# One stage of a decoder trunk: late half projections in other turns, fixed places and other queues for attention's operands, one more turn behind the head norm

## The chip, the cores and the metric

The kernel runs on one core of one Trainium2 chip, as one launch. The metric is the device time of that launch in microseconds (us). The engines are named as in the profile: PE (TensorE, matrix products), PEld (its weight loads), DVE (VectorE), ACT (ScalarE), POOL (GpSimd) and SP (SyncE, which only issues DMAs). Each engine works off its own list of instructions in order; an instruction whose operand isn't ready holds up all that stand behind it on that engine. DMAs are issued from the lists of SP, ACT and POOL, and run beside the engines.

## The reference: what is computed

One layer of a trunk, sequence 1024, width 1024. The part that matters here is the mixing: one input projection of the normed input, split into three groups of heads that are computed apart and projected back together.

```python
z = rmsnorm(h, norm_mix_g[l]) @ w_in[l]
a_q, a_f, a_i, a_g, b_q, b_k, b_v, c_in = jnp.split(z, splits, axis=-1)
o_a = hgrn2_mix(a_q, a_f, a_i, a_g, lbs[l], hgrn_gnorm_g[l])      # 4 heads of 128
o_b = dilated_window_mix(b_q, b_k, b_v)                           # 4 heads of 64, three windows
o_c, v_first = rwkv7_mix(c_in, ...)                               # 4 heads of 64
h = h + jnp.concatenate([o_a, o_b, o_c], axis=-1) @ w_out[l]
h = h + conv_glu_ffn(rmsnorm(h, norm_ffn_g[l]), ...)
h = h + sigmoid(rmsnorm(h, norm_ple_g[l]) @ ple_gate[l]) * (p[l] @ ple_proj[l])
return rmsnorm(h, final_norm_g)
```

HGRN2 is a gated linear recurrence; each head's output is normed by itself (root mean square over its 128 columns), then multiplied by a gate. The attention adds three dilated causal windows under one softmax.

## The kernel before, in words

All activations lie transposed, 128 channels by 1024 positions. A product in full precision is made as three products of rounded parts (`mm3`, L125 to L134): high part by high, low by high, high by low. A weight block arrives as `wraw`, ACT copies its high part (`whi`, L106), DVE or POOL subtracts to get the low part (`wlo`, L108).

**Stages.** `phase_mix` (L308) first does the norm, then RWKV together with most blocks of the input projection, then the stage with which this case deals (L314 to L328), and after it `phase_out`, the output projection (its products are named `dp`), and the gated MLP. In the stage four streams run interleaved: A is the HGRN heads 0 and 2, one after the other, B the heads 1 and 3, C the attention of the two pairs of heads (`swa`), F the three blocks of the input projection that were left over (`project_late`): block 29, which is attention's v for pair 1, block 19, the gate of head 2, and block 23, the gate of head 3.

**Turns.** Each stream is a generator. `interleave` (L68) goes through a string of letters, and each letter lets its stream go on to its next `yield`. The string has rounds: in round r comes C if r is in `TURNS` (0, 1, 3, 4, 6, 7 and so on), then A, then B from round 6 on, then F in the odd rounds below 14 (L326, L327). This gives the order in which the program is written down; a scheduler of the framework then lists it per engine by when it takes operands to be ready, and may move instructions past one another.

**An HGRN head** (`hgrn_head`, L971) has these turns: load of the gate f and of q (`zl<-z`, from SP); first factors; scores of level 0 (`hsc`, L1002); seven levels, each four products of 128 by 128 (`hsc`, L1023), a predicated copy (`hS`, L1025), products with the running gate (`qt` L1028, `hk` L1026) and a copy for the next level (`ks` on ACT, L1013); transposes of v and of the keys (`vt`, L1046 and L1052); states (`hkv` L1067, chained on DVE as `hst`); output (`hpo`, L1086 and L1088); the head norm: square on ACT, sum on DVE, power on POOL (`hrs`, L1098), product on DVE (`ho`, L1100). The last turn transposes the normed output on PE (`vt<-cst,ho`, L1106), multiplies with the gate and splits it into the operand of the output projection.

**Attention** (`swa`, L1113) handles a pair of heads in 10 turns: scores of a query block qb (`swq`, L1167), mask and minimum on DVE (`lg`, L1174), exponential on ACT (L1176), a turn later the transposes of the weights (`swt`, L1190), and after another one the products with v (`swo`, L1203). Its operands q, k, v come back from memory by three DMAs on POOL's list (`swa_load`); v is transposed into `sV` (L1150) before the first scores. The places for q, k, v and `sV` are four buffers under one tag, taken in turn by whichever tile comes next when one is free.

**Late projections.** One turn of F is a half of a block: 24 products of 128 by 512 into one small accumulator `zp`, scaled on DVE, stored by a DMA on SP's list. They need nothing of the other streams. After the sixth half the stream makes the operand tiles of the output projection, which take the places of the input projection's operands X, and splits what is done by then (`o_split`, `xh` on ACT and `xl` on DVE or POOL, L155 and L157).

All small accumulators of the stage (`zp`, `hsc`, `vt`, `hkv`, `hpo`, `swt`, `swo`, `swd`) share four buffers; `swq` and `dp` share two larger ones. The HGRN tiles share 11 buffers.

In the profile, the products in 32 bits (all but those with `whi` and `wlo`) leave two records each, so a row "x8" in the trace is four instructions.

Of the kernel before, what the change touches and what calls it, by code (L numbers as in the profile page):

```python
# [10 lines left out]
F32 = mybir.dt.float32  # L11
# [7 lines left out]
P = 128  # L19
T = 1024  # L20
# [47 lines left out]
def interleave(order, streams):  # L68

    live = dict(streams)  # L70
    while live:
        for s in order:
            if s in live and next(live[s], STOP) is STOP:
                del live[s]
# [5 lines left out]
class Trunk:  # L80
# [227 lines left out]
    def phase_mix(self):  # L308
        nc, tc = self.nc, self.tc
        self.mix_norm()  # L310
        with tc.tile_pool(name="slots", bufs=1) as slots:
            self.slots, self.NSLOT = slots, 8
            self.rwkv()
        self.O, self.done = None, []  # L314
        for p in (0, 1):
            self.o_split(6 + p)
        with tc.tile_pool(name="hg", bufs=1) as slots, tc.tile_pool(name="sw", bufs=1) as sp:
            self.slots, self.NSLOT = slots, 11
            self.hgrn_setup()
            self.sp = sp  # L320
            self.swmask = sp.tile([P, T], F32, name="swmask")
            nc.scalar.dma_start(self.swmask, self.a["swm"])
            A = chain(self.hgrn_head(0), self.hgrn_head(2))
            B = chain(self.hgrn_head(1), self.hgrn_head(3))
            order = []
            for r in range(36):  # L326
                order += "C" * (r in self.TURNS) + "A" + "B" * (r > 5) + "F" * (r % 2 and r < 14)  # L327
            interleave(order, {"A": A, "B": B, "C": self.swa(sp), "F": self.project_late(self.rest)})  # L328

    TURNS = [i * 33 // 22 for i in range(23)]  # L330

    def mix_norm(self):

# [637 lines left out]
    def hgrn_head(self, h):  # L971
        nc, mxp, par, spool = self.nc, self.mxp, self.par, self.spool
# [6 lines left out]
        q = self.zload(j0 + 1, self.slot)  # L979
        yield  # L980
        nc.vector.tensor_scalar(f, f, self.olb[:, h:h + 1], self.lb[:, h:h + 1], ALU.mult, ALU.add)
        k = self.slot("hk")
# [16 lines left out]
        for i in (0, 1):  # L999
            sc = mxp.tile([P, 4, P], F32, tag="mx", name=self.nm("hsc"))  # L1000
# [5 lines left out]
        def blocks(l):  # L1006
            n = 1 << (l - 1)
            return n, HT // n, ([HT + n, 2], [2 * n, 256 // n], [1, n])
# [9 lines left out]
        for l in range(1, 8):  # L1018
            n, nb, half = blocks(l)
            qq = view(qt, 0, *half)  # L1020
            sc = mxp.tile([P, 4, P], F32, tag="mx", name=self.nm("hsc"))
# [19 lines left out]

        V = self.slot("hV")
        for hf in (0, 1):
            pt = mxp.tile([P, HT], F32, tag="mx", name=self.nm("vt"))
            for c in range(4):
                nc.tensor.transpose(pt[:, c * P:(c + 1) * P], vc[:, hf * HT + c * P:hf * HT + (c + 1) * P], self.ident)  # L1046
            nc.scalar.copy(V[:, hf * HT:(hf + 1) * HT], pt)
        kt = self.slot("hkt")
# [8 lines left out]
        def at(cc, swap=False):  # L1057
            c = (4 + cc if cc < 4 else 7 - cc) ^ (4 if swap else 0)
            return slice(c * P, (c + 1) * P)

        for hf in (0, 1):
            pk = mxp.tile([P, 4, P], F32, tag="mx", name=self.nm("hkv"))
            for c in range(4):
                cc = hf * 4 + c
                if cc == 7:
                    break
                nc.tensor.matmul(pk[:, c, :], kt[:, at(cc, True)], V[:, at(cc)], start=True, stop=True)  # L1067
            for c in range(4):
# [12 lines left out]
        for hf in (0, 1):  # L1081
            po = mxp.tile([P, 4, P], F32, tag="mx", name=self.nm("hpo"))
            for c in range(4):
                cc = 7 - c if hf == 0 else c
                s = at(cc)
                nc.tensor.matmul(po[:, c, :], S[:, s], V[:, s], start=True, stop=cc == 0)  # L1086
                if cc:
# [11 lines left out]
        o3 = o.rearrange("p (c v) -> p c v", v=P)  # L1099
        nc.vector.tensor_tensor(o3, o3, rs.unsqueeze(2).broadcast_to([P, 8, P]), ALU.mult)  # L1100
        yield
        for hf in (0, 1):
            sl = slice((1 - hf) * HT, (2 - hf) * HT)
            pt = mxp.tile([P, HT], F32, tag="mx", name=self.nm("vt"))
            for c in range(4):
                nc.tensor.transpose(pt[:, c * P:(c + 1) * P], o3[:, hf * 4 + c, :], self.ident)  # L1106
            nc.vector.scalar_tensor_tensor(oa[:, sl], pt if hf else pt[:, ::-1], par[:, PC_GN + h:PC_GN + h + 1], oa[:, sl], ALU.mult, ALU.mult)
# [4 lines left out]

    def swa(self, sp):  # L1113

        pend, fin, load = [], None, self.swa_load(sp, 0)
        yield
        for p in (0, 1):
            d = load
            self.swa_values_in(d)
            for qb in range(10):  # L1120
                if fin:
                    self.swa_out(*fin)
                    fin = None
                if qb < 8:
                    cur = self.swa_scores(sp, d, qb)
                if qb > 1:
                    fin = self.swa_values(sp, d, *pend.pop(0))
                if 0 < qb < 9:
                    pend[-1:] = [self.swa_turn(sp, *pend[-1])]
                if qb < 8:  # L1130
                    pend.append((qb, *cur))
                if qb == 7 and p == 0:
                    load = self.swa_load(sp, 1)
                yield
        self.swa_out(*fin)

    def swa_load(self, sp, p):
        d = {"p": p}
        for i, n in enumerate("qkv"):
            d[n] = self.zload(24 + 3 * p + i, lambda n: sp.tile([P, T], F32, tag="sslot", name=self.nm(n), bufs=4),  # L1140
                              self.nc.gpsimd)
        return d

    def swa_values_in(self, d):
        nc, vc = self.nc, d["v"]
        V = self.sp.tile([P, T], F32, tag="sslot", name=self.nm("sV"), bufs=4)
        for hf in (0, 1):
            pt = self.mxp.tile([P, HT], F32, tag="mx", name=self.nm("vt"))
            for c in range(4):
                nc.tensor.transpose(pt[:, c * P:(c + 1) * P], vc[:, hf * HT + c * P:hf * HT + (c + 1) * P], self.ident)  # L1150
            nc.scalar.copy(V[:, hf * HT:(hf + 1) * HT], pt)
        d["V"] = V.rearrange("p (b c) -> p b c", c=P)

# [699 lines left out]
```

## Time and profile before

| | us |
|---|---|
| median of 3 runs (1495.39 to 1498.95) | 1496.69 |
| the profiled execution, its own time | 1496.24 |
| its span from first to last instruction | 1494.5 |
| PE busy | 1445.1 (97%) |
| DVE busy | 1097.8 (73%) |
| ACT busy | 634.5 (42%) |
| POOL busy | 446.6 (30%) |
| the 16 DMA engines moved | 167.83 MB, 112 GB/s on the mean |

The stage starts at about 433.7 us of the span, and the operands of the output projection are all there at about 649 us. How to read a row of the timeline: start, length, engine, line, operation, output<-inputs, shape, number of instructions merged, and in brackets how long the engine was idle before it and what ended that. "PEclk" is the clock that PE was granted, as a share of the full one.

### The profile page before, as it was taken

The page shows a single profiled execution, that of the slowest core. Times are in us where ns is not written, and L with a number is a line of the kernel's source. Part 1 is how long each engine was busy: PE and PEld are TensorE (multiplying, and loading weights), DVE is VectorE, ACT ScalarE, POOL GpSimd, SP SyncE. Part 2 cuts the span into 40 slices and gives each one's busy share as a digit, 9 for nine tenths or more (in the row PEclk, how much of TensorE's full clock was granted, in tenths as well). Part 3 has the DMA queues.
Part 4 walks back from the last instruction along what each step waited for, and adds up shares of the span by engine and source line. Part 5 has one row for each costly group of instructions (what it writes and reads, how often), then busy time and mean ns, then how long its engine had stood idle before and what let it go on. Part 6 is the DMA issues. An engine that isn't in the chain of part 4 may idle for free.

```text
span 1494.5 us, 20176 instructions
## 1 busy us (share of the span) xinstructions
PE 1445.1 (97%) x7416; PEld 1199.0 (80%) x7416; DVE 1097.8 (73%) x1650; ACT 634.5 (42%) x1121; POOL 446.6 (30%) x362
## 2 busy tenths in 40 slices
PE   8999999999989889999999999999999999999996
PEld 7888997888977677778878888888888888888775
DVE  7666455585648668736788888888888799777684
ACT  6531343213425635425454444444444444455542
POOL 3232432313412122112144554444554000002343
PEclk9999999999999989999999999999999999999998
DMA  6123112232152111165333333333332883351443
GB/s 219 58 92 99 43 56 72 72 99 63 43 179 74 42 73 57 43 229 194 127 110 98 103 106 106 106 106 106 106 106 81 313 298 97 105 164 42 139 157 106
DMA packets 79874, 167.83 MB, mean 112 GB/s; under 512 B 20064, under 2 KB 22240, under 8 KB 79776
## 3 DMA queue, kind: packets, MB, share of 16 engines
q1 hardware_dynamic: 65424, 145.44, 29.8%
q10 hardware_dynamic: 13264, 17.04, 3.4%
q0 software_dynamic: 1088, 4.06, 0.8%
q8 instruction: 58, 0.95, 0.3%
q14 instruction: 40, 0.33, 0.1%
HBM read 120.12 MB, written 46.40 MB: 111 GB/s over the span
## 4 chain that ended last, share of the span: by engine, by line
PE 84%; DVE 6%; issue 4%; POOL 2%; DMA 2%; ACT 1%; DVEq 0%; POOLq 0%; ACTq 0%; SPq 0%
PE bg L1325 16%; PE bv L1325 12%; PE dp L130 8%; PE dp L134 8%; PE dp L132 8%; PE bg L1626 7%; PE bv L1626 7%; PE hsc L1023 2%; DMA zl<-z 1%; PE swq L1167 1%; PE swo L1203 1%; POOL wlo L108 1%; PE bv L130 1%; PE bv L132 1%; PE swt L1190 1%
## 5 line engine op out<-in xcount | busy, mean ns | idle before, releaser
L130 PE MATMUL dp<-xh,whi 128*128 128x512 f32 x560 | 202.7, 406 | 1.1 <-ACT xh L374 1.1
L134 PE MATMUL dp<-xh,wlo 128*128 128x512 f32 x560 | 194.4, 391 | 2.0 <-POOL wlo L108 1.1
L132 PE MATMUL dp<-xl,whi 128*128 128x512 f32 x560 | 194.5, 391 | 0.4 <-DVE xl L375 0.3
L108 POOL TENSOR_TENSOR wlo<-raw,whi 128x512 fp32r<-128x512 f32 x84 | 138.0, 1662 | 77.8 <-ACT whi L106 77.8
L108 POOL TENSOR_TENSOR wlo<-wraw,whi 128x512 fp32r<-128x512 f32 x64 | 88.0, 1379 | 233.2 <-ACT whi L106 203.9
L1325 PE MATMUL bg<-t,whi 128*128 128x512 f32 x352 | 132.7, 389 | 0.0
L106 ACT CAST whi<-wraw 128x512 fp32r<-128x512 f32 x120 | 72.1, 617 | 132.7 <-PE dp L132 94.4
L134 PEld LDWEIGHTS dp<-xh,wlo 128*128 128x128 f32 x560 | 105.0, 188 | 25.0 <-POOL wlo L108 1.5
L130 PEld LDWEIGHTS dp<-xh,whi 128*128 128x128 f32 x560 | 104.5, 188 | 23.6 <-issue 3.8
L132 PEld LDWEIGHTS dp<-xl,whi 128*128 128x128 f32 x560 | 105.2, 188 | 21.8 <-DVE xl L375 1.4
L108 POOL TENSOR_TENSOR wlo<-s,whi 128x512 fp32r<-128x512 f32 x44 | 65.9, 1498 | 159.5 <-ACT whi L106 147.3
L1626 PE MATMUL bg<-t,whi 128*128 128x512 f32 x308 | 95.0, 389 | 0.0
L1626 PE MATMUL bv<-t,whi 128*128 128x512 f32 x308 | 94.8, 389 | 0.0
L106 ACT CAST whi<-raw 128x512 fp32r<-128x512 f32 x88 | 52.6, 619 | 97.4 <-PE bv L1325 49.0
L106 ACT CAST whi<-s 128x512 fp32r<-128x512 f32 x66 | 38.9, 620 | 120.7 <-PE bg L1325 113.3
L1325 PEld LDWEIGHTS bg<-t,whi 128*128 128x128 f32 x352 | 66.0, 188 | 13.6
L175 POOL TENSOR_TENSOR rst<-rst,mhalf 128x4 f32<-128x4 f32 (+1 forms) x9 | 9.8, 1088 | 223.4 <-DVE rst L173 223.4
L108 DVE TENSOR_TENSOR wlo<-wraw,whi 128x512 fp32r<-128x512 f32 x56 | 48.2, 863 | 34.8 <-ACT whi L106 32.4
L1622 ACT CAST t<-t 128x512 fp32r<-128x512 f32 x77 | 47.8, 622 | 47.8 <-PE bv L1626 34.8
L1626 PEld LDWEIGHTS bv<-t,whi 128*128 128x128 f32 x308 | 57.8, 188 | 12.1
L1626 PEld LDWEIGHTS bg<-t,whi 128*128 128x128 f32 x308 | 57.7, 188 | 12.0
L1325 PE MATMUL bg<-t,wlo 128*128 128x512 f32 x176 | 67.2, 389 | 0.0
(429 smaller groups left out, 3660.9 us busy)
## 6 DMA issues: line engine op xcount, KB each, us to landing
raw<-in_ffn_up_dram SPq DMA_DIRECT2D x44, 512.0 KB, 3.7
wraw<-in_w_in_dram SPq DMA_DIRECT2D x29, 512.0 KB, 3.6
z<-zst SPq DMA_DIRECT2D x19, 512.0 KB, 2.9
gb<-ct SPq DMA_DIRECT2D x33, 256.0 KB, 2.0
t<-gb SPq DMA_DIRECT2D x33, 256.0 KB, 2.8
t<-gt SPq DMA_DIRECT2D x33, 256.0 KB, 2.7
zl<-z SPq DMA_DIRECT2D x16, 512.0 KB, 3.5
wraw<-in_ple_gate_dram SPq DMA_DIRECT2D x16, 512.0 KB, 3.6
```

The source lines that it names most:

```text
L106: nc.scalar.copy(hi, src)
L108: eng.tensor_tensor(lo, src, hi.bitcast(F32), ALU.subtract)
L130: nc.tensor.matmul(ps[hf], wh, xh[hf], start=first, stop=False)
L132: nc.tensor.matmul(ps[hf], wh, xl[hf], start=False, stop=False)
L134: nc.tensor.matmul(ps[hf], wl, xh[hf], start=False, stop=last)
L1023: nc.tensor.matmul(sc[:, c, :], ks[:, c * P:(c + 1) * P], view(qt, c * P, [2 * n, 64 // n], [HT + n, 2], [1, n]), start=True, stop=True)
L1167: nc.tensor.matmul(pq[h][:, b:b + w], d["q"][hs, qb * P:nk], d["k"][hs, b:b + w], start=True, stop=True)
L1190: nc.tensor.transpose(pt[:, kb * P:(kb + 1) * P], lg[:, b + kb * P:b + (kb + 1) * P], self.ident)
L1203: nc.tensor.matmul(po[hs, :], d["V"][:, kb, hs], pT[h][:, kb * P:(kb + 1) * P], start=kb == 0, stop=kb == qb)
L1325: nc.tensor.matmul(ps, w[part == 2][:, s], X[k][part == 1], start=start and k == part == 0, stop=k == 3 and part == 2, skip_group_check=no ...
L1622: nc.scalar.copy(xh, x)
L1626: nc.tensor.matmul(ps[m], wt[part == 2][:, m * P:(m + 1) * P], (xh, xl)[part == 1], start=k == part == 0, stop=k == NK - 1 and part == 2)
```

## The change

The reads of the four streams stay what they were; their places in the order, the places of attention's operands and the queues of its loads are others:

- The F turns stand in rounds 0, 1, 5, 9, 13, 16 and 17 (`LATE`) in place of 1, 3, 5, 7, 9, 11 and 13.
- The head norm's last turn comes one `yield` later, so that a head takes one round more, and the string has 38 rounds.
- Attention's q, k, v and `sV` have a buffer of their own each (`sa`, `sb`, `sc`, `sd`; the second pair's k goes to `sc`, its q to `sa`, its v to `sb`). The second pair's k is loaded from POOL's list after query block 5 of the first pair, q from ACT's list and v from POOL's list after block 7. `sV` is made after the scores of the first query block for pair 0, and after those of the second for pair 1.
- The pools `hg` and `sw` are opened so that each of their tiles waits for the earlier users of its own bytes only.

```diff
-        with tc.tile_pool(name="hg", bufs=1) as slots, tc.tile_pool(name="sw", bufs=1) as sp:
+        with self.pool("hg") as slots, self.pool("sw") as sp:
...
-            for r in range(36):
-                order += "C" * (r in self.TURNS) + "A" + "B" * (r > 5) + "F" * (r % 2 and r < 14)
+            for r in range(38):
+                order += "C" * (r in self.TURNS) + "A" + "B" * (r > 5) + "F" * (r in self.LATE)
...
+    LATE = 0, 1, 5, 9, 13, 16, 17
...
         nc.vector.tensor_tensor(o3, o3, rs.unsqueeze(2).broadcast_to([P, 8, P]), ALU.mult)
         yield
+        yield
...
-        pend, fin, load = [], None, self.swa_load(sp, 0)
+        nc, pend, fin = self.nc, [], None
+        ds = {0: {"p": 0}, 1: {"p": 1}}
+        for n, tag in zip("qkv", ("sa", "sb", "sc")):
+            self.swa_load(ds[0], n, tag, nc.gpsimd)
         yield
         for p in (0, 1):
-            d = load
-            self.swa_values_in(d)
+            d = ds[p]
...
                     cur = self.swa_scores(sp, d, qb)
+                if qb == p:
+                    self.swa_values_in(d)
...
-                if qb == 7 and p == 0:
-                    load = self.swa_load(sp, 1)
+                if p == 0 and qb == 5:
+                    self.swa_load(ds[1], "k", "sc", nc.gpsimd)
+                if p == 0 and qb == 7:
+                    self.swa_load(ds[1], "q", "sa", nc.scalar)
+                    self.swa_load(ds[1], "v", "sb", nc.gpsimd)
...
-    def swa_load(self, sp, p):
-        d = {"p": p}
-        for i, n in enumerate("qkv"):
-            d[n] = self.zload(24 + 3 * p + i, lambda n: sp.tile([P, T], F32, tag="sslot", name=self.nm(n), bufs=4),
-                              self.nc.gpsimd)
-        return d
+    def swa_load(self, d, n, tag, eng):
+        d[n] = self.zload(24 + 3 * d["p"] + "qkv".index(n),
+                          lambda nm: self.sp.tile([P, T], F32, tag=tag, name=self.nm(nm), bufs=1), eng)
...
-        V = self.sp.tile([P, T], F32, tag="sslot", name=self.nm("sV"), bufs=4)
+        V = self.sp.tile([P, T], F32, tag="sd", name=self.nm("sV"), bufs=1)
```

On PE the two lists differ only between row 1606 and row 2180 of 5267, which is this stage; in front of and behind it they are word for word the same. The lines of the changed kernel are numbered higher by 1 up to L1100, and by up to 6 behind it. Three places show what moved.

The first is PE's list at the start of the stage: `yt` and `pg` are the last products of RWKV, `vt` with `sV`'s operand `zl_3698` the transposes of v for pair 0, `zp` the half projection. Before:

```order
L751 MATMUL yt_3665<-cst,sc_2353 128x128 x4
L755 MATMUL pg_3672<-sg_474,par 128x512
L1150 MATMUL vt_3705<-cst,zl_3698 128x128 x4
L1150 MATMUL vt_3711<-cst,zl_3698 128x128 x4
L1167 MATMUL swq_3718<-zl_3696,zl_3694 128x128
L1167 MATMUL swq_3719<-zl_3696,zl_3694 128x128
L130 MATMUL zp_3746<-xh_105,whi_3736 128x512
```

In the changed kernel, the same place:

```order
L752 MATMUL yt_3665<-cst,sc_2353 128x128 x4
L756 MATMUL pg_3672<-sg_474,par 128x512
L130 MATMUL zp_3716<-xh_105,whi_3706 128x512
L132 MATMUL zp_3716<-xl_106,whi_3706 128x512
L134 MATMUL zp_3716<-xh_105,wlo_3708 128x512
```

The first half projection (24 products) now stands right behind RWKV; behind it come the two scores and the transposes of v, then the second half projection, and only then the scores of head 0's level 0, ahead of which one half projection stood before.

The second place is PE's list where the first pair of attention ends and head 0's output begins: `swt` are transposes of the weights of query block 6, `swq` the first scores of pair 1, with k and q in its inputs (`zl_4396`, `zl_4394` before, `zl_4100`, `zl_4326` now). Before:

```order
L1190 MATMUL swt_4383<-cst,lg_4211 128x128 x4
L1190 MATMUL swt_4389<-cst,lg_4211 128x128 x3
L1167 MATMUL swq_4629<-zl_4396,zl_4394 128x128
L1167 MATMUL swq_4630<-zl_4396,zl_4394 128x128
L1167 MATMUL swq_4712<-zl_4396,zl_4394 128x256
L1167 MATMUL swq_4713<-zl_4396,zl_4394 128x256
L1086 MATMUL hpo_4401<-hV_4250,hS_3773 128x128
```

Now:

```order
L1196 MATMUL swt_4315<-cst,lg_4172 128x128 x4
L1173 MATMUL swq_4533<-zl_4100,zl_4326 128x128
L1196 MATMUL swt_4321<-cst,lg_4172 128x128 x3
L1087 MATMUL hpo_4331<-hV_4211,hS_3800 128x128
L1089 MATMUL hpo_4331<-hst_4248,qt_3771 128x128
```

One score product of pair 1 is left ahead of head 0's output; the other three come 80 rows and more behind it. Ahead of these pieces stood, before, the sixth half projection, the last two scores of pair 0 and 12 `swo`; now the two scores and 12 `swo` alone.

The load of that q is the third place. Before, k and v of pair 1 stood on POOL's list behind three pieces that split operands (`zl_800` is k, `zl_801` is v; q, `zl_799`, had gone far earlier):

```order
L157 TENSOR_TENSOR xl_833_4507<-oc_286_1640,xh_832_4506 128x512
L108 TENSOR_TENSOR wlo_1071_5630<-wraw_1065_5622,whi_1070_5628 128x512
L157 TENSOR_TENSOR xl_835_4509<-oc_567_3267,xh_834_4508 128x512
L502 DMA zl_800_4396<-z28_3663 128x1024
L502 DMA zl_801_4398<-z29_3745 128x1024
L1098 TENSOR_TENSOR hrs_817_4480<-hss_816_4477,mhalf_83 128x8
```

Now k takes the early place on POOL's list, and q stands on ACT's list, between copies for head 1's levels and the exponential of query block 7:

```order
L1014 COPY ks_778_4273<-hk_728_4024 128x2x32x8
L1014 COPY ks_796_4358<-hk_728_4024 128x2x16x16
L503 DMA zl_790_4326<-z27_3620 128x1024
L1182 ACTIVATE lg_781_4282,sden_716_3977<-lg_781_4282,sden_716_3977 128x1024
```

The load of q waits for the last scores of pair 0, whose buffer it takes, and ACT waits with it. The transposes of head 0's normed output (`vt<-cst,ho`), too, have moved on PE's list: before, they came after 14 `swo`, 16 `swt` and one level; now a half projection, another level and 16 `swo` more stand between head 0's output and them. Of the other two half projections the fourth stands between levels of head 1 as one did before, and the last behind head 1's transposes.

## The prediction

> **What bounds the kernel now.** I read the page first, then the busy time of each engine by windows in the stage that the change rewrites, then what PE waits for there, and last the single rows. The page:
>
> ```profile
> span 1494.5 us, 20176 instructions
> ...
> PE 1445.1 (97%) x7416; PEld 1199.0 (80%) x7416; DVE 1097.8 (73%) x1650; ACT 634.5 (42%) x1121; POOL 446.6 (30%) x362
> ```
>
> PE is busy for 97% of the span, and the change leaves its instructions as they are. What can be won is PE's idle time and the time in which it runs at a lowered clock. The windows of the stage (start:end, length, then each engine's busy time with its count, the granted clock, the DMA share, GB/s) show where these lie:
>
> ```profile
> 433.70:462.84 29.14, 23.52 (x123) 18.45 (x122) 20.09 (x43) 10.74 (x27) 6.23 (x7) 0.94 0.49 163
> 462.84:514.50 51.66, 51.54 (x338) 40.47 (x337) 35.19 (x70) 31.94 (x57) 7.47 (x6) 1.00 0.11 37
> 514.50:550.06 35.56, 24.81 (x199) 21.59 (x199) 18.75 (x32) 15.51 (x29) 9.71 (x9) 0.81 0.33 111
> 550.06:634.40 84.34, 78.03 (x634) 62.81 (x633) 69.60 (x134) 44.22 (x92) 18.52 (x15) 0.98 0.13 45
> ...
> 433.70:650.00 216.30, 191.66 (x1363) 154.59 (x1362) 150.81 (x289) 105.88 (x207) 46.07 (x39) 0.95 0.21 71
> ```
>
> The first and the third stretch hold the holes: 5.6 and 10.8 us idle of 24.6 in all. In the second PE never waits. The clock fell to half in four places:
>
> ```profile
> 445.60:449.00 3.40, 3.40 (x18) 3.40 (x18) 1.95 (x5) 0.40 (x2) 0.21 (x1) 0.50 0.99 314
> 524.10:530.90 6.80, 5.54 (x24) 4.63 (x25) 1.05 (x6) 0.88 (x4) 0.00 (x0) 0.50 0.25 103
> 541.20:548.00 6.80, 5.49 (x34) 5.29 (x36) 5.68 (x8) 1.24 (x2) 1.82 (x3) 0.50 0.01 2
> 575.30:578.70 3.40, 3.37 (x18) 2.74 (x19) 3.30 (x6) 0.27 (x1) 0.00 (x0) 0.50 0.08 14
> ```
>
> At half rate half of PE's busy time is lost: (3.40 + 5.54 + 5.49 + 3.37) / 2 = 8.9 us. Without any hole the stage would be 24.6 + 8.9 = 33.5 us shorter; no change of order can give more. PE's waits in the stage (us in total, times, longest):
>
> ```profile
> PE vt L1106 <- DVE ho L1100: 8.0, 3, 4.4
> PE swq L1167 <- DMA zl<-z: 5.3, 1, 5.3
> PE hsc L1002 <- DVE hk L984: 3.7, 1, 3.7
> PE hsc L1023 <- DVE qt L1028: 3.4, 4, 1.6
> ```
>
> **The change, part by part.** All sums are made against the profiled execution's own 1496.24 us; the median is 0.45 higher, and about 0.2% (3.0 us) is the least that a measurement tells from no change.
>
> *a. The start, up to the third half projection.* The same work stands ahead of it as before, but the second half comes ahead of level 0's scores and covers their wait.
>
> ```profile
> 435.14 0.50 PE L130 MATMUL zp<-xh,whi 128*128 128x512 f32 x1
> ...
> 440.48 0.39 PE L134 MATMUL zp<-xh,wlo 128*128 128x512 f32 x1
> ...
> 461.95 1.13 PE L1023 MATMUL hsc<-qt,ks 128*128 128x128 f32 x8 [1.65 <-DVE qt L1028]
> ```
>
> A half projection lasts about 5.5 us (435.14 to 440.7), more than the 3.72 idle. At most 3.72 + 1.65 and 1.7 us of lost clock go, 7.1 in all. But DVE must then do the factors and both levels in the shorter time:
>
> ```profile
> 443.00:461.90 18.90, 14.83 (x74) 11.71 (x74) 16.54 (x33) 7.11 (x19) 4.39 (x4) 0.91 0.35 116
> ```
>
> It is busy 16.54 of these 18.90 us, so it gives up some 2.4 us, and about 1 us more from starting on its work while PE projects. I take +3.3 (0 to 7.1).
>
> *b. The middle (462.84 to 514.5).* One half projection that hid a level's turnaround there is now used up at the start, so levels follow each other with only attention's products between. The one uncovered level above waited 1.65 us. A gain is excluded (PE idles 0.12 us there); at worst the 8 levels wait 1.65 each, 13 us. DVE has 35.19 of 51.66 us of work, so it isn't full; I take −1.5 (−13 to 0).
>
> *c. Attention's operands.* Before, q and k of pair 1 were there late:
>
> ```profile
> 518.69 1.01 PE L1190 MATMUL swt<-cst,lg 128*128 128x128 f32 x7 [0.69 <-DVE zst L474]
> 525.01 0.80 PE L1167 MATMUL swq<-zl,zl 64*128 64x128 f32 x4 [5.31 <-DMA zl<-z]
> 526.16 1.43 PE L1167 MATMUL swq<-zl,zl 64*128 64x256 f32 x4 [0.35 <-DVE sden L1174]
> ```
>
> With half of 5.54 at the lowered clock that hole costs 0.69 + 5.31 + 0.35 + 2.8 = 9.1 us. Now k comes early and q's load goes out, from ACT, when the last scores of pair 0 end. ACT waits there too, but what is queued behind it (the exponential of query block 7) needs those very scores, so this wait is costed at nothing. Between those scores and q's first use PE has 12 `swo` and 11 of 14 `swt`:
>
> ```profile
> 515.55 1.53 PE L1203 MATMUL swo<-pT,sV 128*64 128x128 f32 x24
> 517.01 0.98 PE L1190 MATMUL swt<-cst,lg 128*128 128x128 f32 x7
> ```
>
> That is 1.5 and, for 11 of two such groups, 1.5: 3.0 us. The load of 512 KB is priced by the medians from issue to landing:
>
> ```profile
> zl<-z SPq DMA_DIRECT2D x16, 512.0 KB, 3.5
> ...
> swmask<-in_swm_dram ACTq DMA_DIRECT2D x1, 512.0 KB, 5.1
> ```
>
> and, of the two loads that made the hole, on POOL's list:
>
> ```profile
> zl<-z POOLq DMA_DIRECT2D x2, 512.0 KB, 7.5
> ```
>
> I take 5.1, the only one from ACT's list: 2.1 us stay open, with 0.35 behind. Whether the clock falls after so short a hole, one row shows:
>
> ```profile
> 575.33 1.94 PE L1106 MATMUL vt<-cst,ho 128*128 128x128 f32 x8 [1.81 <-DVE ho L1100]
> ```
>
> 1.81 us idle, and the stretch 575.3 to 578.7 ran at 0.50; so 1.7 us more are lost. The gain is 9.1 − 2.1 − 0.35 − 1.7 = +5.0. With 3.5 it is up to 8.6 (9.1 − 0.5), with 7.5 it is 1.8 (4.5 open, 2.8 of clock).
>
> The Trainium skill ("TensorE: Matmul & The Clock Gate", section "Why this matters for your kernels") advises against idle gaps of over some 3 us, since one window of idle brings the clock to half. By that rule a hole of 2.1 us would keep the clock, the gain would be 6.7 and the forecast 1479.3; the trace's 1.81 us with half the clock behind it speaks against it, and the row decides.
>
> *d. Head 0's norm.* PE's last `hpo`, what it did until it had to wait, and the wait:
>
> ```profile
> 532.36 0.39 PE L1088 MATMUL hpo<-hst,qt 128*128 128x128 f32 x2
> 532.59 1.06 PE L1023 MATMUL hsc<-qt,ks 128*128 128x128 f32 x8
> 533.57 1.75 PE L1203 MATMUL swo<-pT,sV 128*64 128x128 f32 x28
> 535.25 1.97 PE L1190 MATMUL swt<-cst,lg 128*128 128x128 f32 x16
> 537.05 1.06 PE L1023 MATMUL hsc<-qt,ks 128*128 128x128 f32 x8
> 542.51 1.94 PE L1106 MATMUL vt<-cst,ho 128*128 128x128 f32 x8 [4.40 <-DVE ho L1100]
> ```
>
> The norm takes 532.7 to 542.5, 9.8 us; cover was 5.4. Now a half projection (5.5), a level (1.0) and 16 `swo` (14 took 1.75, so 2.0) come on top: 13.9 us, 4 more than needed. The hole of 4.40 and half of 5.49 go, 7.1 us; I keep 0.7 for a small accumulator that isn't free yet (0.69 is what such a wait cost at 518.69): +6.4 (2.7, if as long a wait comes at the levels, to 7.1). If that cover failed, 4.4 + 2.7 would be back.
>
> *e. Head 1's norm.* Its last `hpo` and one of the score products behind it:
>
> ```profile
> 567.55 0.39 PE L1088 MATMUL hpo<-hst,qt 128*128 128x128 f32 x2
> ...
> 568.98 1.13 PE L1167 MATMUL swq<-zl,zl 64*128 64x512 f32 x4
> ```
>
> From its end at 567.8 to `vt` at 575.33 are 7.5 us, of which PE worked 5.7. Now some 7.0 us of PE's work lie between: three levels (3.2 by the 1.06 above), 6 `swo` (0.75) and 10 `swt` (1.2) by the rows of head 0, and three long and two short `swq` (some 1.9, the long ones half of 1.13 each). The wait of 1.81 with its 1.7 of clock could go whole, 3.5; DVE is 83% busy in this stretch (69.60 of 84.34), so I take +2.0 (0 to 3.5).
>
> *f. The rest.* The last two halves lie among head 1's and head 2's levels. A table switch more on ACT:
>
> ```profile
> 515.60 1.28 ACT L472 ACT_TABLE_LOAD   x1
> ```
>
> ACT is busy 44.22 of 84.34 us there, so these 1.28 us are hidden; if ACT were what PE waits for, they would cost 1.3 each. The operand splits (`xh`) are listed on ACT behind F's last products and may be held up some us; PE needs them only at the end. The pools' finer waits let SP's loads go earlier, which no PE row waits for. The last head's norm keeps its hole (8.0 − 4.40 − 1.81 = 1.8 us). I take 0 (−4 to +3).
>
> Sum: 3.3 − 1.5 + 5.0 + 6.4 + 2.0 + 0 = 15.2; 1496.24 − 15.2 = **1481.0 us**.
>
> **The rivals.**
>
> *R1: q's load is no shorter than before.* Then c gives 1.8 in place of 5.0, for 1484.2. For it: the two loads that made the hole took 7.5 us. Against it: two ran side by side, now k has gone ahead, and v goes with q. The Trainium skill ("DMA: Bandwidth & Descriptors", section "Issuing engines are not separate DMA queues") says that transfers of all issuers share the same 16 engines and that another issuer saves only the time to issue. The medians of one size, 3.5 on SP's list and 7.5 on POOL's, are against it as far as they go; no row shows such a load on ACT's list. 0.20.
>
> *R2: nearly all holes close.* a, c and e at their upper ends, b at 0: 7.1 + 8.6 + 6.4 + 3.5 = 25.6, 1470.6. For it: the stretch 462.84 to 514.5 shows that the streams can cover one another fully. Against: DVE in the first stretch. 0.09.
>
> *R3: DVE sets the pace.* If levels wait for its products with the running gate, then a is 0, b −4, e 0 and f −4, with c and d kept: 3.4, about 1493. For it: the four `hsc` waits on `qt`, 3.4 us. Against: DVE has 65 us of slack in 216. 0.10, of which 0.06 lies within 3.0 us of no change.
>
> *R4: slower.* With two halves spent at the start, the levels of heads 0 and 1 stand uncovered: seven levels that each wait 1.65 and lose 1.7 of clock cost 23.5, which eats the 16.7 of a, c, d and e, for about 1503. It decides from 16.7 / 7 = 2.4 us a level on. Against: attention's products lie between, and a row of them (1 to 2 us above) covers most of the wait. 0.06.
>
> **How the numbers follow.** The forecast's case has 0.55. Its unknown costs, b and c above all, give some 7 us to either side; 1471 to 1491 takes in R1 and the edge of R2 and leaves out R4 and most of R3. Faster 0.55 + 0.20 + 0.09 + 0.04 = 0.88, same 0.06, slower 0.06.
>
> **What would show it.** Right: no DMA among PE's waits over 2.5 us; `vt` behind head 0's norm with no wait; PE's idle time in the stage near 15 us in place of 24.6 and about 4 in place of 8.9 lost to the clock. Wrong: `hsc` waits on `qt` of over 8 us in all (R3, R4), or `swq` waiting 4 us or more on `zl<-z` (R1). PE idle outside the stage must stay as it is.

## The result, and the profile after

The changed kernel takes 1488.61 us (median of 5 runs, 1487.04 to 1491.58) where the kernel before, in 5 runs beside it, takes 1498.38: a ratio of 0.9942, with a 95% interval of 0.9927 to 0.9958. It is faster, inside the range: by the ratio 8.7 us where 15.2 were forecast (the medians lie 9.8 us apart, the two profiled executions 7.6). The profiled execution took 1488.61 us, with a span of 1486.8. The page of the changed kernel:

```profile
span 1486.8 us, 20174 instructions
...
PE 1446.8 (97%) x7416; PEld 1199.0 (81%) x7416; DVE 1100.6 (74%) x1650; ACT 634.5 (43%) x1121; POOL 448.8 (30%) x361
```

To see where the time went, the span is cut at two steps that both kernels have: the end of the last transposes of a normed head output (`vt<-cst,ho`, the end of the stage), and the first sums of the norm behind the output projection (`ps_ss`). The first window starts when RWKV's last product is done. Windows of the kernel before, with the columns as in the prediction:

```profile
433.81:646.01 212.20, 187.63 (x1348) 151.84 (x1347) 148.46 (x287) 104.64 (x205) 44.66 (x38) 0.95 0.21 70
646.01:697.57 51.56, 50.56 (x221) 40.91 (x220) 22.99 (x31) 15.95 (x27) 11.70 (x9) 1.00 0.72 255
697.57:1494.45 796.88, 779.19 (x3467) 644.01 (x3465) 662.63 (x841) 360.94 (x555) 255.76 (x168) 0.99 0.39 128
```

The same three of the changed kernel:

```profile
433.67:632.12 198.45, 182.82 (x1351) 147.01 (x1350) 152.01 (x288) 104.29 (x205) 45.81 (x36) 0.98 0.21 72
632.12:686.32 54.20, 51.73 (x217) 41.40 (x217) 22.84 (x31) 16.16 (x27) 12.31 (x9) 0.97 0.71 252
686.32:1486.75 800.43, 783.23 (x3467) 646.79 (x3465) 662.64 (x841) 360.98 (x555) 255.27 (x168) 0.99 0.39 128
```

The stage is 13.75 us shorter, PE's idle time in it went from 24.6 to 15.6. Then 2.64 us are lost in the output projection and 3.55 in the rest, on which no edit bears: −0.14 (start) − 13.75 + 2.64 + 3.55 = −7.70, the difference of the spans. In the rest PE isn't idle longer (17.7 before, 17.2 after); it is busy longer on the same work, which is a lower clock (the last section shows the two places).

PE's waits from 420 to 660 us of the changed kernel:

```profile
PE hsc L1024 <- DVE qt L1029: 5.3, 6, 1.7
PE swt L1196 <- ACT ob L1210: 2.8, 2, 1.8
PE dp L130 <- ACT whi L106: 2.3, 1, 2.3
PE hsc L1024 <- DVE hS L1005: 1.9, 1, 1.9
PE vt L1108 <- DVE ho L1101: 1.7, 1, 1.7
```

The wait for the DMA is gone, and of the three waits for a normed head only the last head's is left. New is a wait of the output projection for its weights' high part (`whi`, 2.3 us). `swt` waits twice, 2.8 us in all where it was 0.9 once, for `ob`, ACT's copy of attention's output out of a small accumulator. The rows behind these, in PE's timeline:

```profile
458.67 0.48 PE L130 MATMUL zp<-xh,whi 128*128 128x512 f32 x1
...
505.37 0.66 PE L1196 MATMUL swt<-cst,lg 128*128 128x128 f32 x4 [1.80 <-ACT ob L1210]
505.95 0.48 PE L1173 MATMUL swq<-zl,zl 64*128 64x128 f32 x2
...
525.41 0.66 PE L1108 MATMUL vt<-cst,ho 128*128 128x128 f32 x4 [0.60 <-DVE hS L1026]
...
561.05 1.13 PE L1024 MATMUL hsc<-qt,ks 128*128 128x128 f32 x8 [1.60 <-DVE qt L1029]
562.02 1.04 PE L1108 MATMUL vt<-cst,ho 128*128 128x128 f32 x8
...
653.84 0.50 PE L130 MATMUL dp<-xh,whi 128*128 128x512 f32 x1 [2.32 <-ACT whi L106]
```

### The profile page after: what moved, and what is told of

It is laid out like the page before. It is cut to its first block, busy times and chain, and to the rows that moved or that the text cites. A ratio compares the mean times of both kernels' runs of the same rounds, so it can differ in the third digit from the quotient of the medians.

```text
span 1486.8 us, 20174 instructions
## 1 busy us (share of the span) xinstructions
PE 1446.8 (97%) x7416; PEld 1199.0 (81%) x7416; DVE 1100.6 (74%) x1650; ACT 634.5 (43%) x1121; POOL 448.8 (30%) x361
## 4 chain that ended last, share of the span: by engine, by line
PE 83%; DVE 6%; issue 4%; POOL 3%; ACT 2%; DMA 1%; DVEq 0%; ACTq 0%; SPq 0%; POOLq 0%
PE bg L1331 16%; PE bv L1331 12%; PE dp L130 8%; PE dp L134 8%; PE dp L132 8%; PE bg L1632 7%; PE bv L1632 7%; PE hsc L1024 1%; PE swq L1173 1%; POOL wlo L108 1%; PE bv L130 1%; PE bv L134 1%; PE bv L132 1%; PE swt L1196 1%; DVE qt L1029 1%
```

## The experiments

All are compared in one table. Ratio is to the kernel before, timed beside it; the three columns of us are of one profiled execution each, cut as above. "Stage and projection" runs from RWKV's last product to the norm's sums.

| kernel | ratio, 95% interval | stage | stage and projection | rest |
|---|---|---|---|---|
| before | 1 | 212.2 | 263.8 | 796.9 |
| changed | 0.9942 [0.9927, 0.9958] | 198.5 | 252.7 | 800.4 |
| changed, once more | 0.9927 [0.9914, 0.9941] | 196.5 | 250.6 | 800.4 |
| F turns alone | 0.9903 [0.9884, 0.9921] | 195.8 | 247.3 | 796.8 |
| F turns, pools | 0.9896 [0.9880, 0.9912] | 196.7 | 248.2 | 798.0 |
| places alone | 0.9946 [0.9931, 0.9962] | 203.3 | 255.1 | 796.7 |
| extra turn alone | 1.0049 [1.0035, 1.0063] | 215.5 | 269.5 | 798.4 |
| changed without extra turn | 0.9944 [0.9927, 0.9961] | 198.6 | 250.4 | 801.8 |
| changed with old places | 0.9941 [0.9928, 0.9955] | 200.4 | 254.4 | 801.0 |
| changed with old F turns | 0.9960 [0.9947, 0.9974] | 203.4 | 257.6 | 798.4 |
| changed, q from POOL's list | 0.9929 [0.9912, 0.9946] | 202.2 | 256.4 | 798.5 |
| changed, pools exchanged | 0.9942 [0.9926, 0.9958] | 207.6 | 255.0 | 799.8 |
| changed, mask below | 0.9956 [0.9943, 0.9969] | 200.4 | 254.6 | 802.1 |
| changed, other order on ACT | 0.9945 [0.9926, 0.9964] | 199.3 | 254.0 | 799.7 |

The theory at this point: the four parts act as the terms of the sum did (turns a, b and part of d; places c; extra turn d and e), and the loss behind the stage comes from the burst of loads there. The rivals are in the expectations.

### The changed kernel with one part undone

The old F turns:

```diff
-    LATE = 0, 1, 5, 9, 13, 16, 17
+    LATE = 1, 3, 5, 7, 9, 11, 13
```

> The changed kernel with the F turns in the old rounds (1, 3, 5, 7, 9, 11, 13), all else new. If the parts act as the prediction's terms do: PE's hole ahead of head 0's level 0 is back (3.7 us idle, half clock behind it), about 4 us, and behind head 0's output only some 9 us of other work stand ahead of the transposes of the norm's 9.8, so a wait of about 1 us, with or without half clock, comes back there. Time 4 to 7 us above the changed kernel's. Rival (the turns are worth nothing, places and the extra turn bring it all): within 1.5 us of the changed kernel. The first weights of the MLP still wait for the last operand split, so the wait of the output projection (2.3 us, half clock behind it) stays.

Measured: 4.9 us above the changed kernel from the stage's start to the norm's sums (257.6 against 252.7), as expected, but not for the reasons given. The hole ahead of head 0's level 0, which I expected back with 3.7 us, isn't there: these scores begin at 440.63 without a wait (why, the run with the places alone shows below). The largest of PE's waits are now `hsc` for `qt`, 10.4 us in all and 5.2 the longest: behind head 0's output the hole isn't at the norm's transposes but at the level ahead of them. The ratios, 0.9960 and 0.9942, lie only 2.7 us apart, and their intervals overlap; the interval of the changed kernel's second comparison (0.9914 to 0.9941, below) lies wholly under this one.

Without the extra turn:

```diff
         nc.vector.tensor_tensor(o3, o3, rs.unsqueeze(2).broadcast_to([P, 8, P]), ALU.mult)
         yield
-        yield
```

> The changed kernel without the extra turn behind the head norm. Head 0's norm is still covered by the half projection (10.9 us of work for 9.8). Head 1's norm loses cover: about 1.8 us idle, perhaps 1.7 of clock. Without the extra turn the gate of the last head lies in another of the HGRN buffers, and the first of the MLP's four weight loads is free ahead of the last operand split as before. If the give-back behind the stage comes from that, PE's wait in the output projection falls from 2.3 us with half clock to about 0.9 without, 3 us less, and the kernel is within 2 us of the changed one. Rival (the give-back comes from the earlier start of the burst, whatever the places): that wait stays at 2 us or more, and the kernel is 2 to 4 us slower than the changed one.

Measured: the ratio is that of the changed kernel. The output projection's window is 51.7 us in place of 54.2 and holds no wait over 0.9. So the loss in the output projection belongs to the extra turn, and the stage itself isn't slower without it (198.6 against 198.5). Whether the loss goes by the places, as I had written, is tried below.

q from POOL's list, with `nc.gpsimd` for `nc.scalar` at its load:

> The changed kernel with q of pair 1 loaded from POOL's list, all else the same. If the queue matters: the load is issued about 0.7 us later and lands 5 to 7.5 us after its issue in place of 3.5, PE waits 1 to 3 us at the first scores of pair 1, time 1 to 5 us above the changed kernel's. If only the place and the moment matter (the transfer is as long from any list): landing near 3.5 us, no DMA among PE's waits over 0.5 us, within 1 us of the changed kernel.

Measured: no DMA among PE's waits at all. The loads from POOL's list took 4.4 us (median of two) where ACT's had taken 3.5, and PE had to wait 1.8 us at that point anyway, for ACT's copy `ob`, which stands on ACT's list behind the exponential of query block 7. PE's idle time up to the norm's sums is 18.8 us against 18.1; the rest of the stage's 3.7 us more is clock, and the ratio is no worse. The queue doesn't matter here.

The two pools exchanged in memory:

```diff
-        with self.pool("hg") as slots, self.pool("sw") as sp:
+        with self.pool("sw") as sp, self.pool("hg") as slots:
```

> The changed kernel with the two pools of the stage exchanged in memory: attention's below, HGRN's above. The MLP's first four weight loads and the eight loads of the residual then take places that attention used, and can go out while the last HGRN heads are still at work. If the gain that the stage made is given back by the burst of loads behind it: PE's wait of 2.3 us in the output projection and the half clock behind it go, 3 to 4 us, perhaps a little more since DVE's and ACT's work on these loads moves up too. Time 3 to 5 us below the changed kernel's. Rival (the wait in the output projection comes from the weights of the output projection themselves, which have other places): the wait stays, within 1 us of the changed kernel.

Measured: behind the last head PE doesn't wait any more:

```profile
641.20:688.64 47.44, 47.44 (x209) 38.91 (x209) 21.77 (x31) 16.80 (x27) 11.63 (x9) 1.00 0.60 208
```

The window is 6.8 us shorter than the changed kernel's, and the stage 9.1 longer, partly because products of the projection have moved into it (the counts are 209 and 1360 for 217 and 1351). The gain is paid for at the other end: attention's first operands now lie where RWKV's tiles were, and PE's waits have a new row, `swq` for `zl<-z`, 3.9 us. In sum nothing is won.

### One part of the change alone

The places and queues of attention's operands in the kernel before (the part of the diff in `swa`, `swa_load` and `sV`'s tile):

> The kernel before with the new places and queues of attention's operands alone (turns, head norm and pools as before). By term c: the wait of 5.3 us for the load of pair 1 and the two small ones beside it go, and the half clock behind them; 6 us of PE's idle time and up to 2.8 of clock, the other holes (3.7 at the start, 4.4 at head 0's norm) stay. Time 6 to 9 us below the kernel before. Rival (the transfer is as long as before, 7.5 us): 1 to 3 us below.

Measured: 8.6 us less up to the norm's sums, no DMA among PE's waits. That is the size of term c, but by luck, for the gain comes about in another way. Up to head 0's last output product this kernel gains 12.5 us, of which 4.8 lie at the start: the wait of 3.7 us ahead of head 0's level 0, which I expected to stay, is gone with the F turns where they were. DVE's first factor of head 0, in the kernel before and in this one:

```profile
443.04 0.81 DVE L981 TENSOR_SCALAR zl<-zl,olb,lb 128x1024 f32<-128x1024 f32 x1 [6.70 <-DMA zl<-z]
```

```profile
438.98 0.82 DVE L981 TENSOR_SCALAR zl<-zl,olb,lb 128x1024 f32<-128x1024 f32 x1 [2.00 <-DMA zl<-z]
```

So the hole at the start was a wait for the load of head 0's gate. It is issued at about the same moment in both (435.4 and 435.7), but here ahead of a weight's load and of one of attention's in place of behind them, and lands 4 us earlier. The load of q, from ACT's list, took 7.4 us here, about as long as the two from POOL's list before (7.5); PE doesn't wait for it since the scores that need it now stand behind head 0's output (they begin at 525.71, q landed at 522.34). Behind head 1's norm a half-clock stretch of 10.2 us takes part of the gain back.

The extra turn in the kernel before:

> The kernel before with the extra turn behind the head norm alone. Between head 0's output and the transposes of its norm a level and 16 of attention's products more than before, 8.4 us of work for 9.8: PE's wait there falls from 4.4 to 1.4 us or less, with or without half clock. The last head's gate takes the place of the first of the MLP's weights, so the wait in the output projection rises from 0.9 to 2.3 us with half clock, 3 us more. Net 0 to 3 us below the kernel before. Rival (the extra turn is what covers the norm, the half projection isn't needed, and the places cost nothing): 5 us below or more.

Measured: slower, by a ratio of 1.0049, where I expected 0 to 3 us less. PE's waits of this kernel from 430 to 690 us:

```profile
PE hsc L1023 <- DVE qt L1028: 12.0, 6, 5.6
PE swq L1168 <- DMA zl<-z: 4.9, 1, 4.9
PE hsc L1002 <- DVE hk L984: 4.7, 2, 3.9
PE dp L130 <- ACT whi L106: 2.3, 1, 2.3
PE vt L1107 <- DVE ho L1100: 1.7, 1, 1.7
```

The wait of `vt` for the norm is down from 8.0 to 1.7, and that of `hsc` for `qt` up from 3.4 to 12.0. Its 5.6 us are the level that now stands ahead of the transposes. PE and DVE there:

```profile
544.77 2.05 PE L1023 MATMUL hsc<-qt,ks 128*128 128x128 f32 x8 [5.61 <-DVE qt L1028]
...
550.01 1.09 PE L1107 MATMUL vt<-cst,ho 128*128 128x128 f32 x8
```

```profile
541.35 2.07 DVE L1100 TENSOR_TENSOR ho<-ho,hrs 128x1024 f32<-128x1024 f32 x1 [1.56 <-POOL hrs L1098]
543.34 0.71 DVE L1025 COPY_PREDICATED hS<-cmask,hsc 128x512 f32<-128x512 uint8 x1
543.95 0.67 DVE L1028 TENSOR_TENSOR qt<-qt,hT 128x512 f32<-128x512 f32 x1
```

DVE works in order: the product with the norm (`ho`) waits for POOL's power, and the level's copy and its `qt` stand behind it. A level put between the norm and its transposes needs the same DVE, so it waits as long as the transposes did. It is no cover. A half projection needs nothing of DVE, and is.

The F turns in the kernel before:

> The kernel before with the F turns in the new rounds alone. The hole at the start closes (about 4 us with its clock), the norm of head 0 is covered by the half projection (10.9 us for 9.8, up to 7 us with its clock). Attention's load is still late: its wait stays at 4 to 6 us. The last head's gate stays where it was, so the wait in the output projection stays at 0.9. Time 7 to 11 us below the kernel before. Rival (a half projection taken from the middle opens waits for the running gate there): less than 4 us below, and PE's waits of hsc for qt above 8 us.

Measured: 16.5 us less up to the norm's sums, a ratio of 0.9903 (14.5 us, where I expected 7 to 11): more than the whole change brings. And the DMA wait, of which I expected 4 to 6 us, isn't there. POOL's list shows why, here in the timeline of this kernel:

```profile
500.65 1.08 POOL L1027 TENSOR_TENSOR hk<-hk,hT 128x512 f32<-128x512 f32 x1 [13.70 <-ACT ks L1014]
501.67 1.12 POOL L503 DMA_DIRECT2D zl<-z  x2
515.51 2.15 POOL L1099 TENSOR_TENSOR hrs<-hss,mhalf 128x8 f32<-128x8 f32 x1 [12.73 <-DVE hss L1097]
```

PE's last scores of pair 0 end at 501.0, and the two loads are issued 0.7 us later; they landed in 4.0 us (median). In the kernel before, those scores ended at 515.6, and POOL was still at the splits of operands that F's sixth turn had put on its list; it issued the loads at 518.3, and they took 7.5 us beside the store and the loads of the same turn. What made attention's operands late was the F turn: its splits ahead of the loads, and its transfers beside them. The queue alone doesn't shorten the load: q from ACT's list took 7.4 us in the run with the places alone and 6.7 in the one with the old F turns, and 3.5 in the changed kernel, where no F turn stands there.

The finer waits of the pools, with the F turns:

> The kernel before with the new F turns and the finer waits of the two pools alone; the order of every engine is that of the turns alone. If the pools' waits count for nothing: 247 to 248 us from the start of the stage to the norm's sum, as with the turns alone, and 13 to 16 us below the kernel before. If they bring loads forward that matter: 1 us less or better.

Measured: 248.2 us up to the norm's sums, a ratio of 0.9896. The pools count for nothing that can be told. This and the F turns alone are the fastest of the study. The interval that the changed kernel had in its first comparison (from 0.9927) lies wholly above theirs; that of its second (0.9914 to 0.9941) overlaps the one of the F turns alone (0.9884 to 0.9921) and not the one with the pools (to 0.9912).

The changed kernel with the old places and the old queue:

> The changed kernel with attention's operands in the old places and on the old queue, so the new turns, the extra turn and the pools alone. If the new turns by themselves bring attention's load forward (POOL's splits of operands no longer stand ahead of it): no DMA among PE's waits over 0.5 us, and the time within 2 us of the changed kernel's. If the places and queues carry their 6 us here too: that wait is back at 3 to 6 us, and the kernel is 4 to 8 us slower than the changed one.

Measured: no DMA among PE's waits, and the ratio of the changed kernel. On top of the new turns the places bring nothing that can be told.

### The loss behind the stage

Places first. In the changed kernel the gate of the last head lies where the first of the MLP's four weight loads must go; in the kernel before it didn't. Moving all HGRN buffers by one tile puts two of the four loads into free places:

```diff
-        with self.pool("hg") as slots, self.pool("sw") as sp:
+        with self.pool("swm") as sm, self.pool("hg") as slots, self.pool("sw") as sp:
...
-            self.swmask = sp.tile([P, T], F32, name="swmask")
+            self.swmask = sm.tile([P, T], F32, name="swmask")
```

> The changed kernel with attention's mask placed below the HGRN buffers instead of above, which moves them by one tile, all else the same: now two of the MLP's four first weight loads take places that are free before the last head's norm. If the give-back behind the stage is the burst of loads that this place delays: the 2.3 us wait in the output projection and the half clock behind it go, from the end of the stage to the norm's sum 51 to 52.5 us in place of 54.2, and the kernel is 2 to 3 us faster than the changed one, with the stage itself as before (198.4 us). Rival (the burst is too big for two loads to matter): 54 us there, no difference.

Measured: SP issued its first `raw` load at 627.4, ahead of the last head's end (634.8), and still 54.2 us and the wait of 2.3. What PE waited for had itself waited for PE here, not for a load: the square of the residual's third block 3.70 us for DVE's sum, and that sum 4.15 us for PE's products. The burst of loads isn't the cause; that theory falls.

What all kernels with the extra turn share but the one with the pools exchanged, and none without it has, is the order that the scheduler writes down for ACT and DVE at that point. ACT's list in the kernel before (`sqt` is the square of a block of the residual, `whi_5668` the high part that PE waited for in the changed kernel):

```order
L106 CAST whi_5664<-wraw_5662 128x512
L106 CAST whi_5668<-wraw_5662 128x512
L106 CAST whi_5704<-wraw_5702 128x512
L1245 DMA hd_0_5471<-h_5461 128x512
L200 ACTIVATE sqt_5659<-h_5461 128x512
```

In the changed kernel the store and the square, which need PE's products and DVE's sum of the third block, come ahead of the second `whi`; on DVE, two sums of squares come ahead of the low parts (`wlo`). To try ACT's part alone:

```diff
-                nc.scalar.dma_start(self.hd[m][g], u)
+                (nc.sync if (m, g) == (2, 0) else nc.scalar).dma_start(self.hd[m][g], u)
...
-            nc.scalar.activation(t, src, AF.Square)
+            if on_dve:
+                nc.vector.tensor_tensor(t, src, src, ALU.mult)
+            else:
+                nc.scalar.activation(t, src, AF.Square)
```

> The changed kernel with one step of the output projection taken off ACT's list: the square of the third block of the residual is done on DVE, and its store is issued by SP. So the high part of the next weights (whi) stands on ACT right behind the one before, as it did in the kernel before, and no longer behind that square, which waits for PE's products. If the 2.3 us that PE waits in the output projection come from this order on ACT: that wait and the half clock behind it go, from the end of the stage to the norm's sum 51 to 52.5 us in place of 54.2, time 2 to 3 us below the changed kernel's. Rival (the wait comes from the burst of loads): 54 us stay.

Measured: not so. The wait for `whi` is gone, and in its place PE waits for the low part:

```profile
PE dp L134 <- DVE wlo L108: 3.2, 1, 3.2
```

The square that I had put on DVE took 1.75 us there, ahead of `wlo`. So ACT's order isn't what sets the end alone; the splits of the weights stand behind work on the residual on DVE's list too. With the places alone, one sum of squares stands ahead of a low part on DVE, and PE waits 1.5 us for `wlo`. Where no such work stands ahead on either list, PE waits 0.9 us (the kernel before) or not at all (pools exchanged). That it takes both is consistent with these runs, but a kernel that mends both and nothing else was not run, so this stays argued.

### The changed kernel once more

> The changed kernel once more, unchanged, for the spread of its clock. From the start of the stage to the norm's sum 252.6 us as before if that part is settled by the order; the rest of the program, whose work no edit touches, between 796.8 and 802 us, according to whether PE's gap of 1.6 us there is followed by half clock. If the clock goes by the program, that gap is followed by half clock again; if by chance, as likely not.

Measured: 250.6 up to the norm's sums and 800.4 behind, with half clock behind the gap of 1.6 us again. So one kernel's stage differs by 2 us between two executions (198.5 and 196.5): in the first, an `hsc` waited 1.9 us at 450.85 and the clock fell behind it, in the second neither.

## Why the prediction was right, and where it wasn't

The range held, the direction held, and the saving is 8.7 us for 15.2. The signs held too: no DMA among PE's waits, 0.6 us at the transposes behind head 0's norm, 15.6 us of PE idle in the stage, and 3.4 us lost there to half clock. The stage gave 13.75 us, near the forecast; most of what is missing was lost behind it. By the prediction's own steps, from the rows of the profiles before and after, where work that moved across a cut is taken out (a half projection at 5.7 us):

- **a**, +3.3: the third half projection starts at 458.67 instead of 462.84; less the 0.14 of the start, +4.0. The size is about right, but the reading left something out: ahead of its factors DVE had waited 6.70 us for the load of head 0's gate, which the prediction doesn't name, and its own work filled only the last 2.2 us ahead of level 0. Now this load lands 2 us earlier (440.96 for 443.02), and the second half covers the time behind it.
- **b**, −1.5: from there to head 0's transposes of v, 40.7 us with three halves before, 35.9 with two now: −0.9. The levels weren't left bare; rival R4 is out.
- **c**, +5.0: from those transposes to head 0's last output product 29.2 us before, 15.7 now; without the sixth half and the three score products (1.0) that moved, +6.9. q's load took 3.5 us and was hidden. The 1.8 us that PE waited were for `ob`, behind the exponential on ACT's list, and no half clock followed. The prediction had costed ACT's waiting there at nothing; the same 1.80 us stand where q's load is on POOL's list, so the load on ACT isn't what costs them. R1 is out, though not by the queue: where the sixth F turn stays, q's load takes 7.4 and 6.7 us from ACT's list, near the 7.5 of before.
- **d**, +6.4: the wait 4.40 became 0.60, and the 2.75 us of clock went: +6.5.
- **e**, +2.0: the wait of 1.81 and its clock went, a wait of 1.60 at the level ahead came: +1.9.
- **f**, 0 (−4 to +3): what is left of the stage, 13.75 − 18.4 = −4.7. New or longer waits stand at the levels of heads 1 to 3 (0.70 and 1.74 among them) and at `swt` (1.2), and one half-clock stretch at 546.3.
- **Behind the stage**: the prediction said that PE's idle time there must stay as it is. That failed: 2.64 us in the output projection, and 3.55 in the rest by the clock.

So the step that failed is f, taken as 0 for the stage and, by its sign, for all that lies behind: the two lost 4.7 and 6.2 us. PE's list is the same word for word behind the stage, but the lists of ACT and DVE did move there, and PE waits for them. The extra turn brings the loss in the output projection: every kernel with it shows about 54 us there but the one with the pools exchanged, and every kernel without it 51.5 to 51.9.

The sum also took the right amounts for the wrong parts. The F turns alone do a, c and d. Places and queues alone do a and c as well (4.8 and 7.7 us up to head 0's last output product), so that the two together are worth one of them. The extra turn does nothing for d; alone it costs 5.7 us up to the norm's sums. Taken away from the changed kernel it gives back 2.5 us in the output projection, and in the ratio nothing that can be told (0.9944 against 0.9942 and 0.9927). The claim that a level and 16 `swo` would cover the norm counted PE's time only, and left out that the level needs DVE behind the norm's own product: that is the rival that the prediction had as R3, in one place instead of everywhere.

## What to carry to other kernels

Cover for a wait must come from work that needs nothing of the engine that is late; a step that queues behind the same engine only moves the wait one row ahead. When several edits aim at one hole, try each alone: here one of four brought it all, one brought half of it again, and one cost time, and only their sum was to be seen in the profile. And an order that is "the same" on the busiest engine says nothing of the engines that feed it.

## What the runs showed of the hardware

The clock steps on a fixed grid. The half-clock stretches of the changed kernel start at 450.74, 546.31, 655.54, 1399.64 and 1440.60; these lie 28, 32, 218 and 12 times 3.413 us apart (another begins at 1474.7 and runs to the end). In all 14 profiles the starts of such stretches fit a grid of 3.413 us to 0.01 us. Each lasts one step of the grid, or a few. Two of them, and the same two places in the program before:

```profile
1399.60:1403.10 3.50, 3.50 (x11) 2.69 (x10) 1.74 (x3) 1.25 (x2) 1.22 (x1) 0.51 0.72 227
1440.60:1444.00 3.40, 3.40 (x10) 2.62 (x9) 2.47 (x4) 0.48 (x2) 1.28 (x1) 0.50 0.76 293
```

```profile
1408.80:1412.20 3.40, 3.40 (x19) 2.99 (x20) 2.64 (x6) 0.86 (x2) 1.44 (x1) 1.00 0.32 91
1451.00:1454.40 3.40, 3.40 (x17) 2.81 (x16) 3.38 (x7) 1.12 (x2) 0.68 (x1) 1.00 0.73 263
```

Over the grid steps at full clock of all 14 profiles, from the stage on: where PE was idle for 1.89 us or more of a step, half clock followed in 39 of 39; below 0.84 us in none of some 4000; between these in 35 of about 150. So a gap costs its own length, and then 1.7 us or nothing by how it falls on the grid: the prediction's 1.81 us row with half clock behind it and the 1.80 us gap at 505.37 without were both right, and neither is a rule. The Trainium skill ("TensorE: Matmul & The Clock Gate", section "What's actually happening") gives a free-running window of 3413 ns, with which these traces agree (the grid of 3.413 us). The advice of the Trainium skill on the same page (section "Why this matters for your kernels"), gaps of no more than some 3 us, is too wide here, since 1.89 us inside one step were enough.

The 3.55 us of the rest are two such steps. The same gap of 1.60 us ahead of the last norm's sums stands in all 14 profiles:

```profile
1397.47 1.05 PE L167 MATMUL bv<-few,acc 128*128 128x1 f32 x8 [1.60 <-DVE acc L201]
```

It was followed by half clock in the nine executions of kernels with the extra turn, and not in the five of kernels without it. In the nine it began within 0.4 us before or 0.7 us after a step of the grid, in the five 1.6 to 2.4 us after one. Each kernel has one profiled execution here, the changed one two; why the gap's place on the grid should go with the extra turn stays open.
